# Cross attention with its reciprocal root begun inside the first query strip, delayed scores and whole sample rows; reciprocal roots by Sqrt and a reciprocal

## The chip, the cores and the metric

The kernel runs on one core of one Trainium2 chip. The engines of the core work side by side and meet only at semaphores: TensorE (PE, with its weight loads shown as PEld), VectorE (DVE), ScalarE (ACT), GpSimd (POOL) and SyncE (SP), which issues nearly all DMAs. The metric is the device time of one launch in microseconds. The kernel before took 2563.21 us, the median of three runs (2562.52 to 2563.56).

## The reference

One layer of a decoder step, on 256 prompt tokens (one sequence) and 64 sample tokens (8 sequences of 8), with d = 2048. Everything is float32.

```python
x += 0.5 * swiglu(rmsnorm(x), 5632 wide)              # ffn1
h = rmsnorm(x);  z = h @ w_in                         # 6144 columns
x += concat(hgrn2(z, 8 heads), conv_module(z)) @ w_out  # mixer; each head ends in an rmsnorm, the conv module in a layernorm
q = (rmsnorm(x) @ wq)                                 # cross attention, 4 heads of 128
s = q @ mk.T * 128**-0.5                              # 256 memory tokens
x += (softmax(s) @ mv) @ wo                           # prompt: mk, mv from mem; samples: from the caches
x += 0.5 * swiglu(rmsnorm(x), 5632 wide)              # ffn2
y = rmsnorm_final(x)
def rmsnorm(x, g): return x * rsqrt(mean(x*x) + 1e-6) * g
```

## The kernel before

Activations lie transposed: 16 tiles of 128 features by 320 tokens (256 prompt, then 64 sample). Every weight is read once. A **unit** is a 128x1024 piece of the weight stream: `load` (L134) has SP issue one 512 KB DMA into `raw` (3 buffers), then `split` (L122) makes two fp32r halves of it, `whi` by a cast on ACT (L123) and `wlo` by a subtraction on DVE (L124), 4 buffers each. `unit` fetches units until 4 are ahead of the one in use, with high priority. `mm3` (L186) then multiplies one 128x128 block: three fp32r matmuls into PSUM, L189 (whi by the high half of the activation), L190 (whi by the low half) and L191 (wlo by the high half). A **strip** (L194) is 16 such blocks, two units, 48 matmuls, into one `acc` tile (4 PSUM buffers). Small matmuls use `sm` tiles (4 more).

A scheduler sets the order of instructions on each engine, from the order of the code, priorities and its own costs. Each engine then runs its list strictly in that order: whatever stands behind an instruction that waits, waits too.

**The root.** An rmsnorm is folded in late: strips run on unnormalised x, and their result is multiplied by r = 1/sqrt(mean x² + eps). `Stat` sums squares: ACT squares each tile (L223), POOL adds it up (L225). `rstd` (L230) sums over the partitions by a matmul with ones (L232; with `tail` the last square is not added on POOL but by a second matmul, L234), and `root` (L202) makes r from it: Ln (L205), Identity for v (L206), Exp of -0.5 Ln (L207) and Square (L208) on ACT, then two DVE instructions of a Newton step (L209, L210). The same `root` is called 15 times: ffn1 (the first, called right after the head strips), the memory norm, the mixer norm, 8 heads (L720), the conv layernorm (L547), the cross attention, ffn2 and the final norm.

**Cross attention** (phase `xattn`, from L757). `qstrip(h)` runs one strip of wq; after the first it makes r, then q = acc * r (L793). The attention is fed into the strips by two queues of generators, `aq` (prompt) and `sq` (samples): `tick` counts mm3 blocks, and with `pace[0] = 2` every second block each queue advances one step (to its next `yield`). `attend(h)` is a prompt head: scores (L804), softmax (`exps`: maximum L779, Exp L782, reciprocal of the sums L785, scaling L811), transposes (L817), a copy (L821), values (L825). `attend_sample(j)` does the samples of heads 2j and 2j+1: 16 score matmuls of 32 rows (L835), in 4 steps of 4; softmax; transposes (L851); a copy (L852); 32 value matmuls (L863), in 8 steps of 4; scaling (L873) and a transpose (L876). The caches come in `kv` tiles (8 buffers): those of the second pair go into the buffers of the first as these come free, by DMAs on SP's one queue, between the loads of `raw`. After the four strips `drain` runs what is left; then the wo stage starts, 16 accumulators of 12 matmuls, each added to x by DVE (L904).

Of the kernel before, what the change touches and what calls it, by code (L numbers as in the profile page):

```python
# [13 lines left out]
AF = mybir.ActivationFunctionType  # L14
# [10 lines left out]
T = NP + NS  # L25
# [41 lines left out]
def hymba(tc, A, O):  # L67
    nc = tc.nc
# [14 lines left out]
    with (  # L83
# [11 lines left out]
        def sm():  # L95
            return tl(pp, [P, 512], F32, "sm", 4)
# [94 lines left out]
            nc.tensor.matmul(out, lo, xh, start=False, stop=last)  # L191
            tick(1)

        def strip(xg, ps):  # L194
            for half in range(2):
                w = unit()
                for kk in range(8):
                    k = half * 8 + kk
                    mm3(ps, w, kk, *xg[k], k == 0, k == KT - 1)


        def root(r, ps, n):  # L202
            v = tl(mp, [P, r.shape[-1]], F32, "sq", 2)
            a = sm()[:, : r.shape[-1]]
            nc.scalar.activation(r, ps, AF.Ln, bias=eps, scale=1.0 / n)  # L205
            nc.scalar.activation(v, ps, AF.Identity, bias=eps, scale=1.0 / n)  # L206
            nc.scalar.activation(r, r, AF.Exp, scale=-0.5)  # L207
            nc.scalar.activation(a, r, AF.Square)  # L208
            nc.vector.scalar_tensor_tensor(a, v, -0.5, a, ALU.mult, ALU.mult)  # L209
            nc.vector.scalar_tensor_tensor(r, a, 1.5, r, ALU.add, ALU.mult)  # L210
# [248 lines left out]
        with phase("mixer") as wk:  # L459
# [278 lines left out]
                pump()  # L738


            stat = Stat()
            xg = []
            for part in range(2):
                if part:
# [12 lines left out]
        with phase("xattn") as ap:  # L757
# [28 lines left out]

            def qstrip(h):
                ps = acc()
                strip(xg, ps[:, :T])
                if h == 0:  # L790
                    roots.append(stat.rstd())
                q = tl(ap, [P, T], F32, "q", XH)
                nc.vector.tensor_tensor(q, ps[:, :T], roots[0], ALU.mult)  # L793
                nc.gpsimd.tensor_copy(
                    restride(qms[h].rearrange("p a b -> p (a b)"), 0, [[128, 2], [40, 4], [1, TS]]),
                    restride(q, NP, [[32, 2], [TS, 4], [1, TS]]),
                )
                qs.append(q)
                os_.append(pair("h"))

            def attend(h):
                ps = sm()
                for j in range(2):
                    nc.tensor.matmul(  # L804
                        ps[:, j * 256 : (j + 1) * 256], qs[h][:, j * P : (j + 1) * P], kT[:, h, :], start=True, stop=True
                    )
                pr = tl(ap, [P, 2, MEM], F32, "pr", 2)
                sums = tl(ap, [P, 2], F32, "sums", 2)
                exps(ps.rearrange("p (a b) -> p a b", a=2), pr, 2, sums)
                for j in range(2):  # L810
                    nc.vector.tensor_scalar(pr[:, j, :], pr[:, j, :], sums[:, j : j + 1], None, ALU.mult)  # L811
                yield
                yield
                pt = sm()
                for mc in range(2):
                    for j in range(2):
                        nc.tensor.transpose(  # L817
                            pt[:, mc * 256 + j * P : mc * 256 + (j + 1) * P], pr[:, j, mc * P : (mc + 1) * P], ident
                        )
                pT = tl(ap, [P, 2, NP], F32, "pT", 2)  # L820
                nc.scalar.copy(pT.rearrange("p a b -> p (a b)"), pt)  # L821
                yield
                po = sm()
                for mc in range(2):
                    nc.tensor.matmul(  # L825
                        po[:, :NP], vM[:, mc, h * P : (h + 1) * P], pT[:, mc, :], start=mc == 0, stop=mc == 1
                    )
                split(os_[h][0][:, :NP], os_[h][1][:, :NP], po[:, :NP])

            def attend_sample(j):  # L830
                ps = sm()
                for i4 in range(4):
                    for c in range(4):
                        h, i = 2 * j + c // 2, (c % 2) * 4 + i4
                        nc.tensor.matmul(  # L835
                            ps[c * 32 : (c + 1) * 32, :MEM],
                            qms[h][:, i, :],
                            kv["ck", j, i // 2][:, ((i % 2) * 2 + c // 2) * MEM : ((i % 2) * 2 + c // 2 + 1) * MEM],
                            start=i4 == 0,
                            stop=i4 == 3,  # L840
                            tile_position=(0, c * 32),
                        )
                    yield
                pr = tl(ap, [P, 1, MEM], F32, "prs", 2)
                sums = tl(ap, [P, 1], F32, "sums1", 2)
                exps(ps[:, :MEM].unsqueeze(1), pr, 1, sums)
                yield
                yield
                pt = sm()
                for mc in range(2):  # L850
                    nc.tensor.transpose(pt[:, mc * P : (mc + 1) * P], pr[:, 0, mc * P : (mc + 1) * P], ident)  # L851
                nc.vector.tensor_copy(  # L852
                    restride(pm, 0, [[P, 8], [40, 4], [1, TS]]), pt[:, :256].rearrange("p (a b c) -> p a b c", a=8, b=4)
                )
                yield
                po = sm()
                for mc in range(2):
                    for i4 in range(4):
                        for c in range(4):
                            i = (c % 2) * 4 + i4  # L860
                            b = mc * 512 + c * 128 + i4 * 32
                            v0 = (i % 2) * 512 + mc * 256 + (c // 2) * P
                            nc.tensor.matmul(  # L863
                                po[c * 32 : (c + 1) * 32, :P],
                                pm[:, b : b + 32],
                                kv["cv", j, i // 2][:, v0 : v0 + P],
                                start=mc == 0 and i4 == 0,
                                stop=mc == 1 and i4 == 3,
                                tile_position=(0, c * 32),
                            )  # L870
                        yield
                on = tl(ap, [P, P], F32, "on", 1)
                nc.vector.tensor_scalar(on, po[:, :P], sums, None, ALU.mult)  # L873
                yield
                pt = sm()
                nc.tensor.transpose(pt[:, :P], on, ident)  # L876
                for c in range(2):
                    h = 2 * j + c
                    split(os_[h][0][:, NP:], os_[h][1][:, NP:], pt[:, c * 64 : (c + 1) * 64])
# [29 lines left out]
        with phase("ffn2") as fp:  # L909
            prev, stat1 = stat, Stat(True)  # L910

            def last(n):
                stat1.add(xs[n])
                nc.scalar.activation(xs[n], xs[n], AF.Copy, scale=norm("final", n))
                if n == 1:
                    warm = cp.tile([P, 1], F32, name="warm")
                    nc.scalar.activation(warm, stat1.total[:, :1], AF.Ln)

            ffn(fp, xg, prev.rstd, last)
            r = stat1.rstd()  # L920
# [151 lines left out]
```

## Time and profile before

| | |
|---|---|
| runs (three) | 2562.52, 2563.56, 2563.21 us; median 2563.21 |
| the profiled execution, its own time | 2563.12 us |
| its span, first to last instruction | 2561.3 us |
| mean granted TensorE clock | 0.996 |
| PE busy | 2530.1 us, 99% of the span, 17300 matmuls |
| DVE, ACT, POOL busy | 1458.9, 1070.1, 98.4 us |
| DMA | 393.18 MB, mean 154 GB/s |
| cross attention, strips | from 1526.1 us on |

"Busy" is the share of time in which an engine has an instruction under way. Matmuls overlap in the pipe: a row of the timeline lasts 0.31 us, but in an undisturbed stream the next one starts 0.147 us later, so the distance between starts is what to look at. In the timeline a row has its start, its duration, engine, line and tiles, and in square brackets the idle time before it with what ended it. A plain float32 matmul shows as two entries (x2). In views by stretch of time each row has, for PE, PEld, DVE, ACT and POOL, busy time and number of instructions, then the granted PE clock (1.00 is full), the DMA share and GB/s.

### The profile page before, as it was taken

What the parts mean: (1) busy time and instruction counts of PE and PEld (TensorE: products, weight loads), DVE (VectorE), ACT (ScalarE), POOL (GpSimd) and SP (SyncE); (2) the same over time, 40 slices, a digit from 0 to 9 for tenths busy, and PEclk for the clock granted to TensorE, in tenths of its full rate; (3) what the DMA queues carried; (4) which work ended last, traced back from release to release, by engine and by line L of the source; (5) the groups of instructions that cost most, each with busy time, mean ns of one, the idle gap of its engine ahead of it and who ended that gap; (6) DMA issues with size and microseconds to landing.
All of it is one profiled execution on the core that took longest, in us unless ns stands there. A gap on an engine that the chain in (4) does not pass through costs nothing.

```text
span 2561.3 us, 41649 instructions
## 1 busy us (share of the span) xinstructions
PE 2530.1 (99%) x17300; PEld 2488.9 (97%) x17300; DVE 1458.9 (57%) x2082; ACT 1070.1 (42%) x1472; POOL 98.4 (4%) x104
## 2 busy tenths in 40 slices
PE   8999999999999999999999999999999999999997
PEld 8999999999999999999999997999999999999997
DVE  7545444444444557898787675644444444444444
ACT  6433333333333355555567554533333333333334
POOL 3100000000000020000000021100000000000002
PEclk9999999999999999999999999999999999999999
DMA  6544444444444446444443554444444444444443
GB/s 217 185 148 152 151 150 148 149 150 151 151 148 149 150 154 209 153 153 149 145 151 119 164 193 146 145 152 150 149 148 150 151 152 149 149 149 152 151 149 107
DMA packets 111214, 393.18 MB, mean 154 GB/s; under 512 B 12593, under 2 KB 16817, under 8 KB 111025
## 3 DMA queue, kind: packets, MB, share of 16 engines
q1 hardware_dynamic: 110880, 390.35, 47.0%
q8 instruction: 136, 2.23, 0.3%
q14 instruction: 54, 0.43, 0.0%
q10 hardware_dynamic: 144, 0.16, 0.0%
HBM read 380.71 MB, written 9.76 MB: 152 GB/s over the span
## 4 chain that ended last, share of the span: by engine, by line
PE 95%; DVE 2%; ACT 1%; issue 1%; DMA 0%; SPq 0%; POOLq 0%; DVEq 0%; ACTq 0%
PE acc L189 30%; PE acc L190 30%; PE acc L191 30%; PE sm L612 1%; DVE xgl L243 1%; DVE wlo L124 1%; PE acc L439 1%; PE acc L441 1%; PE acc L440 1%; PE sm L671 0%; ACT whi L123 0%; DMA raw<-in_w 0%; PE sm L707 0%; ACT L207 0%; DVE x L904 0%
## 5 line engine op out<-in xcount | busy, mean ns | idle before, releaser
L123 ACT CAST whi<-raw 128x1024 fp32r<-128x1024 f32 (+1 forms) x689 | 721.7, 1048 | 1363.5 <-PE acc L190 987.5
L124 DVE TENSOR_TENSOR wlo<-raw,whi 128x1024 fp32r<-128x1024 f32 (+1 forms) x689 | 849.0, 1232 | 540.9 <-ACT whi L123 540.4
L189 PE MATMUL acc<-xgh,whi 128*128 128x320 f32 x3616 | 1130.5, 313 | 1.1 <-ACT whi L123 0.7
L191 PE MATMUL acc<-xgh,wlo 128*128 128x320 f32 x3616 | 1119.5, 310 | 1.7 <-DVE wlo L124 1.7
L190 PE MATMUL acc<-xgl,whi 128*128 128x320 f32 x3616 | 1118.8, 309 | 0.5 <-DVE xgl L243 0.4
L189 PEld LDWEIGHTS acc<-xgh,whi 128*128 128x128 f32 x3616 | 680.2, 188 | 7.3 <-issue 4.6
L191 PEld LDWEIGHTS acc<-xgh,wlo 128*128 128x128 f32 x3616 | 680.0, 188 | 2.4 <-DVE wlo L124 1.9
L190 PEld LDWEIGHTS acc<-xgl,whi 128*128 128x128 f32 x3616 | 680.3, 188 | 1.9 <-DVE xgl L243 1.0
L189 PE MATMUL acc<-hh,whi 128*128 128x320 f32 x1728 | 535.3, 310 | 2.1 <-ACT hh L123 1.3
L190 PE MATMUL acc<-hl,whi 128*128 128x320 f32 x1728 | 534.5, 309 | 2.3 <-DVE hl L124 2.3
L191 PE MATMUL acc<-hh,wlo 128*128 128x320 f32 x1728 | 534.1, 309 | 0.0
L189 PEld LDWEIGHTS acc<-hh,whi 128*128 128x128 f32 x1728 | 324.1, 188 | 5.2 <-ACT hh L123 2.8
L190 PEld LDWEIGHTS acc<-hl,whi 128*128 128x128 f32 x1728 | 324.4, 188 | 3.3 <-DVE hl L124 2.8
L191 PEld LDWEIGHTS acc<-hh,wlo 128*128 128x128 f32 x1728 | 324.3, 188 | 0.1
L288 DVE SCALAR_TENSOR_TENSOR x<-acc,x 128x320 f32<-128x320 f32 x192 | 94.1, 491 | 228.2 <-PE acc L191 228.1
L225 POOL TENSOR_TENSOR ssq<-ssq,sq 128x320 f32<-128x320 f32 x73 | 82.1, 1125 | 1867.6 <-ACT sq L223 964.6
L511 DVE SCALAR_TENSOR_TENSOR hl<-u,vec,hl 128x256 f32<-128x256 f32 x240 | 112.5, 478 | 1.8
L249 DVE TENSOR_TENSOR fa<-acc,r 128x320 f32<-128x320 f32 x87 | 42.7, 491 | 108.1 <-PE acc L191 108.0
L257 DVE TENSOR_TENSOR fb<-acc,fa 128x320 f32<-128x320 f32 x87 | 42.7, 491 | 106.9 <-PE acc L191 106.8
L251 DVE TENSOR_TENSOR fa<-fa,r 128x320 f32<-128x320 f32 x88 | 43.7, 497 | 0.1
L124 DVE TENSOR_TENSOR hl<-fb,hh 128x320 fp32r<-128x320 f32 x88 | 42.6, 484 | 0.0
L250 ACT ACTIVATE fa<-fa 128x320 f32<-128x320 f32 x88 | 40.9, 465 | 2.9 <-DVE fa L249 2.7
(208 smaller groups left out, 1055.0 us busy)
## 6 DMA issues: line engine op xcount, KB each, us to landing
raw<-in_w SPq DMA_DIRECT2D x687, 512.0 KB, 3.7
t<-in_s SPq DMA_DIRECT2D x8, 512.0 KB, 4.9
out_ss<-t SPq DMA_DIRECT2D x8, 512.0 KB, 4.1
kv<-in_ck SPq DMA_DIRECT2D x8, 512.0 KB, 5.9
kv<-in_cv SPq DMA_DIRECT2D x8, 512.0 KB, 5.9
mem<-in_mem SPq DMA_DIRECT2D x4, 512.0 KB, 7.3
x<-in_x SPq DMA_DIRECT2D x3, 640.0 KB, 8.0
out_y<-x SPq DMA_DIRECT2D x3, 640.0 KB, 3.1
```

Source lines behind the costliest of these rows:

```text
L123: nc.scalar.copy(hi, src)
L124: nc.vector.tensor_tensor(lo, src, hi.bitcast(F32), ALU.subtract)
L189: nc.tensor.matmul(out, hi, xh, start=first, stop=False)
L190: nc.tensor.matmul(out, hi, xl, start=False, stop=False)
L191: nc.tensor.matmul(out, lo, xh, start=False, stop=last)
L225: nc.gpsimd.tensor_tensor(self.total, self.total, s, ALU.add)
L249: nc.vector.tensor_tensor(t, pg[:, :T], r, ALU.mult)
L250: nc.scalar.activation(t, t, AF.Silu)
L251: nc.vector.tensor_tensor(t, t, r, ALU.mult)
L257: nc.vector.tensor_tensor(h, pu[:, :T], t, ALU.mult)
L288: nc.vector.scalar_tensor_tensor(xs[n], ps[:, :T], 0.5, xs[n], ALU.mult, ALU.add)
L511: nc.vector.scalar_tensor_tensor(dw[:, :NP], u[:, j : j + NP], cw, dw[:, :NP], ALU.mult, ALU.add)
```

## The change

`root` takes Sqrt on ACT and a reciprocal on DVE in place of Ln and Exp on ACT; the Newton step stays. In the cross attention r is made between the two halves of the first strip (with the last square added by the second matmul), the generators of the prompt heads begin 2 steps later (5 for the first), those of the samples 2 steps later, and the 16 score matmuls and 32 value matmuls of a sample pair stand in one step each. A small activation that fetches the last root's table ahead now fetches that of Sqrt.

```diff
-        def strip(xg, ps):
+        def strip(xg, ps, between=None):
             for half in range(2):
+                if half and between is not None:
+                    between()
                 w = unit()
@@ root
-            nc.scalar.activation(r, ps, AF.Ln, bias=eps, scale=1.0 / n)
+            nc.scalar.activation(r, ps, AF.Sqrt, bias=eps, scale=1.0 / n)
             nc.scalar.activation(v, ps, AF.Identity, bias=eps, scale=1.0 / n)
-            nc.scalar.activation(r, r, AF.Exp, scale=-0.5)
+            nc.vector.reciprocal(r, r)
             nc.scalar.activation(a, r, AF.Square)
             nc.vector.scalar_tensor_tensor(a, v, -0.5, a, ALU.mult, ALU.mult)
             nc.vector.scalar_tensor_tensor(r, a, 1.5, r, ALU.add, ALU.mult)
@@ statistics of the cross attention's norm
-            stat = Stat()
+            stat = Stat(True)
@@ qstrip
-                strip(xg, ps[:, :T])
-                if h == 0:
-                    roots.append(stat.rstd())
+                strip(xg, ps[:, :T], (lambda: roots.append(stat.rstd())) if h == 0 else None)
@@ attend
+                for _ in range(5 if h == 0 else 2):
+                    yield
                 ps = sm()
@@ attend_sample
+                yield
+                yield
                 ps = sm()
                 for i4 in range(4):
                     for c in range(4):
                         ...
-                    yield
@@ attend_sample, values
                 for mc in range(2):
                     for i4 in range(4):
                         ...
-                        yield
@@ last
-                    nc.scalar.activation(warm, stat1.total[:, :1], AF.Ln)
+                    nc.scalar.activation(warm, stat1.total[:, :1], AF.Sqrt)
```

The line numbers of the changed kernel are 2 higher from `root` on. The order of instructions moves at three places that the prediction speaks of.

**First root (ffn1), ACT and DVE.** `whi_513`, `wlo_514` and so on are the two halves of the next weight units, `r_482` is the root, `fa` a gate of the ffn. Before, ACT and then DVE:

```order
L205 ACT_TABLE_LOAD
L205 ACTIVATE r_482<-sm_480,eps 128x320
L206 ACTIVATE sq_483<-sm_480,eps 128x320
L207 ACT_TABLE_LOAD
L207 ACTIVATE r_482<-r_482 128x320
L208 ACTIVATE sm_484<-r_482 128x320
L123 CAST whi_513<-raw_512 128x1024
L209 SCALAR_TENSOR_TENSOR sm_484<-sq_483,sm_484 128x320
L210 SCALAR_TENSOR_TENSOR r_482<-sm_484,r_482 128x320
L249 TENSOR_TENSOR fa_491<-sm_122,r_482 128x320
L249 TENSOR_TENSOR fa_501<-acc_124,r_482 128x320
L124 TENSOR_TENSOR wlo_514<-raw_512,whi_513 128x1024
```

With the change:

```order
L207 ACT_TABLE_LOAD
L207 ACTIVATE r_482<-sm_480,eps 128x320
L208 ACTIVATE sq_483<-sm_480,eps 128x320
L123 CAST whi_513<-raw_512 128x1024
L210 ACTIVATE sm_484<-r_482 128x320
L123 CAST whi_519<-raw_518 128x1024
L209 RECIPROCAL r_482<-r_482 128x320
L124 TENSOR_TENSOR wlo_514<-raw_512,whi_513 128x1024
L211 SCALAR_TENSOR_TENSOR sm_484<-sq_483,sm_484 128x320
L124 TENSOR_TENSOR wlo_520<-raw_518,whi_519 128x1024
L212 SCALAR_TENSOR_TENSOR r_482<-sm_484,r_482 128x320
```

The cast of the next unit moved ahead of ACT's Square, and its subtraction from behind two gates to right behind the reciprocal.

**Root of the cross attention, ACT**, from the cast ahead of it to the first Exp (`pr`, `sums`). Before, and behind it the change:

```order
L123 CAST whi_15382<-raw_15381 128x1024
L205 ACT_TABLE_LOAD
L205 ACTIVATE r_15366<-sm_15364,eps 128x320
L206 ACTIVATE sq_15367<-sm_15364,eps 128x320
L207 ACT_TABLE_LOAD
L207 ACTIVATE r_15366<-r_15366 128x320
L208 ACTIVATE sm_15368<-r_15366 128x320
L123 CAST whi_15437<-raw_15436 128x1024
L782 ACTIVATE pr_15396,sums_15397<-sm_15393,mx_2274_15398 128x256 x2
```

```order
L123 CAST whi_15346<-raw_15345 128x1024
L207 ACTIVATE r_15336<-sm_15333,eps 128x320
L208 ACTIVATE sq_15337<-sm_15333,eps 128x320
L210 ACTIVATE sm_15338<-r_15336 128x320
L123 CAST whi_15382<-raw_15381 128x1024
L123 CAST whi_15412<-raw_15411 128x1024
L784 ACT_TABLE_LOAD
L784 ACTIVATE pr_15432,sums_15433<-sm_15429,mx_2277_15434 128x256
L123 CAST whi_15468<-raw_15467 128x1024
L784 ACTIVATE pr_15432,sums_15433<-sm_15429,mx_2277_15434 128x256
```

Both table loads of the root are gone here, and one for Exp has come, behind two casts and ahead of the first Exp.

**PE, the sample values.** `acc_15595` and `acc_15466` are strips. Before, a piece between two of the eight steps (each of the rows of L863 stands there twice), and then the change, where all 32 value matmuls follow one another (each of the four rows eight times):

```order
L863 MATMUL sm_15585<-kv_15283,pm 32x128
L189 MATMUL acc_15595<-xgh_14743,whi_15437 128x320
L190 MATMUL acc_15595<-xgl_14744,whi_15437 128x320
L191 MATMUL acc_15595<-xgh_14743,wlo_15438 128x320
L189 MATMUL acc_15595<-xgh_14782,whi_15437 128x320
L190 MATMUL acc_15595<-xgl_14783,whi_15437 128x320
L191 MATMUL acc_15595<-xgh_14782,wlo_15438 128x320
L863 MATMUL sm_15585<-kv_15281,pm 32x128
L863 MATMUL sm_15585<-kv_15285,pm 32x128
```

```order
L190 MATMUL acc_15466<-xgl_15212,whi_15382 128x320
L827 MATMUL sm_15568<-pT_15556,vM 128x256 x2
L866 MATMUL sm_15573<-kv_15278,pm 32x128
L866 MATMUL sm_15573<-kv_15282,pm 32x128
L866 MATMUL sm_15573<-kv_15280,pm 32x128
L866 MATMUL sm_15573<-kv_15284,pm 32x128
L191 MATMUL acc_15466<-xgh_15211,wlo_15383 128x320
```

Seven of the eight steps of the first pair, and with them seven breaks in the strip, are gone; its score matmuls (L835, now L839) went the same way, from four pieces to one. In the same list the matmuls of the root stand 24 strip matmuls earlier, with one matmul more (L236), and the first scores 9 strip matmuls later in the second strip.

## The prediction

> **What bounds the kernel now.** I read the page's first part, then PE's own waits, then the idle time of PE in stretches of 10 us over the whole span, then the timeline where a stretch had any.
>
> ```profile
> PE 2530.1 (99%) x17300; PEld 2488.9 (97%) x17300; DVE 1458.9 (57%) x2082; ACT 1070.1 (42%) x1472; POOL 98.4 (4%) x104
> PE sm L804 <- DVE q L793: 3.2, 2, 2.6
> PE acc L191 <- DVE wlo L124: 1.7, 1, 1.7
> PE acc L189 <- ACT whi L123: 0.7, 1, 0.7
> 42.80:46.50 3.70, 1.29 (x8) 1.01 (x8) 3.53 (x7) 3.67 (x5) 0.00 (x0) 1.00 0.01 2
> 46.50:49.60 3.10, 3.10 (x13) 3.10 (x13) 3.10 (x5) 1.42 (x3) 0.00 (x0) 0.50 0.84 234
> 1537.80:1540.40 2.60, 0.02 (x2) 0.02 (x1) 1.55 (x4) 1.87 (x3) 0.01 (x1) 1.00 0.19 72
> 1540.40:1545.00 4.60, 4.60 (x19) 4.50 (x20) 2.71 (x6) 1.02 (x4) 1.16 (x1) 0.63 0.33 114
> ```
>
> PE is the bound, so only time in which PE stands still or runs slowly can be won, apart from a tail after its last matmul. PE is idle for 31.2 us of 2561.3 us. Some of that is the start and the tail. Of the rest, two places hang on a root: at 42.8 us (waits of 0.7 and 1.7 us) and at 1537.8 us (2.6 us). Behind each the granted clock is low for 3 to 5 us, 0.50 and 0.63: the halt costs twice, once as a wait and once as 3.10 * 0.50 = 1.55 us and 4.60 * 0.37 = 1.70 us of lost clock.
>
> **The change, part 1: the root.** Each `root` loses an Exp, mostly its table load too, and gains a DVE reciprocal of 320 elements.
>
> ```profile
> L205 ACT ACT_TABLE_LOAD x14 | 18.0, 1283 | 0.2
> L207 ACT ACT_TABLE_LOAD x15 | 19.2, 1283 | 0.3
> L209 DVE SCALAR_TENSOR_TENSOR sm<-sq,sm 128x320 f32<-128x320 f32 x14 | 6.9, 496 | 31.0 <-ACT sm L208 30.9
> L382 DVE RECIPROCAL le<-le x1: 203/203/203, 37.5 to 37.5; 128x8 f32<-128x8 f32 x1
> L785 DVE RECIPROCAL sums<-sums x6: 163/166/167, 1543.6 to 1580.2; 128x2 f32<-128x2 f32 x4, 128x1 f32<-128x1 f32 x2
> ```
>
> The trace has reciprocals of 1, 2 and 8 elements only: 163, 166 and 203 ns. From 2 to 8 is 37 ns, 6.2 ns for each; 166 + 318 * 6.2 = 2.13 us; from 1 to 8 it is 5.7 ns, 1.99 us. I take R = 2.05 us. Bounds: 0.50 us if it runs like the other DVE work on 320 elements (496 ns), 8.1 us if all of the 203 ns grew with the size (40 * 203). The slope speaks for the middle.
>
> [...]
>
> From Sqrt to the Newton step the chain is 0.53 + R + 0.44 with two handovers, 3.1 us, against 3.23 us now (Ln at 2546.53, L209 at 2549.76 in the tail). On DVE, R falls mostly into time in which it already stood idle ahead of L209, 31.0 us over 14 roots, 2.2 us each. So roots that stand off PE's path cost nothing: the memory's, the mixer norm's, ffn2's and those of the heads. If that cover is gone, the next in line is a head's `qk` product, of which the next L612 is in want:
>
> ```profile
> 1149.09 0.48 DVE L616 TENSOR_TENSOR qk<-qk,f 128x320 f32<-128x320 f32 x1
> 1151.97 0.61 PE L612 MATMUL sm<-qk 128*128 128x128 f32 x4
> ```
>
> Here, where DVE has no gap, the product is done 2.4 us early; R pushes it to the edge, not over it. The conv norm's root has two halts behind it:
>
> ```profile
> 1397.37 0.71 PE L189 MATMUL acc<-hh,whi 128*128 128x320 f32 x3 [1.17 <-ACT hh L123]
> 1399.47 0.41 PE L190 MATMUL acc<-hl,whi 128*128 128x320 f32 x1 [1.39 <-DVE hl L124]
> ```
>
> I let it keep its time within 0.3 us: its next unit's cast and subtraction stand ahead of the Newton step now, and lose what the table load gave. I count 0, bounds -0.5 and +0.5 us.
>
> **Part 2: the first root, where the unit behind it comes earlier.**
>
> ```profile
> 39.35 0.53 ACT L205 ACTIVATE r<-sm,eps 128x320 f32<-128x320 f32 x1 [0.75 <-PE sm L232]
> 39.77 0.52 ACT L206 ACTIVATE sq<-sm,eps 128x320 f32<-128x320 f32 x1
> 42.49 1.03 ACT L123 CAST whi<-raw 128x1024 fp32r<-128x1024 f32 x1
> 42.51 0.31 PE L191 MATMUL acc<-xgh,wlo 128*128 128x320 f32 x1
> 44.52 1.22 DVE L124 TENSOR_TENSOR wlo<-raw,whi 128x1024 fp32r<-128x1024 f32 x1
> 45.79 0.41 PE L191 MATMUL acc<-xgh,wlo 128*128 128x320 f32 x1 [1.66 <-DVE wlo L124]
> ```
>
> Now the cast waits for Ln, table load, Exp and Square. With the change it follows Identity: 40.3 to 41.3. The reciprocal runs from 39.9 to 42.0, the subtraction from 42.0 to 43.2, and its first reader, due three matmul steps after 42.51 (43.0), starts at 43.25 in place of 45.79: 2.5 us won. With 0.3 us of halt left there is no slow stretch behind: another 1.5 us. **4.0 us**; bounds 0 (something else holds the unit) and 4.4 us (R = 0.5). The casts behind it are free, their units having been loaded long before (cast there without a DMA wait).
>
> **Part 3: the cross attention.**
>
> ```profile
> 1528.17 1.03 POOL L225 TENSOR_TENSOR ssq<-ssq,sq 128x320 f32<-128x320 f32 x1 [2.49 <-ACT sq L223]
> 1533.14 0.70 PE L232 MATMUL sm<-ssq,ones 128*128 128x320 f32 x2
> 1533.82 0.31 PE L190 MATMUL acc<-xgl,whi 128*128 128x320 f32 x1
> 1539.84 0.49 DVE L793 TENSOR_TENSOR q<-acc,r 128x320 f32<-128x320 f32 x1
> ```
>
> The root's matmuls move from 1533.14 to 24 steps after the strip's start, 1529.6; the last square no longer passes POOL. Sqrt 1530.8 (no table load in the list here), DVE's subtraction ahead of it until 1532.0, reciprocal until 1534.0, Square, Newton until 1535.5, the next unit's subtraction, q at 1537.3 in place of 1540.3. The scores stand 9 steps later, which with the strip before comes to 1539.5: the wait of 2.6 us ends, and the one of 0.6 us at the third head too, 9 steps more lying there as well (L804, 3.2 us in two). With them the slow stretch: 1.7 us. The new Exp table load, 1.28 us like the others, stands behind a cast at 1538 and is done before the scores' maximum (1541.4). The extra matmul of the root costs PE 0.5 us (the one now: 1533.14 to 1533.82, less a step of 0.15).
>
> The samples:
>
> ```profile
> 1550.72 0.31 PE L191 MATMUL acc<-xgh,wlo 128*128 128x320 f32 x1
> 1550.96 0.64 PE L835 MATMUL sm<-kv,qm 128*32 128x256 f32 x8
> 1551.53 0.41 PE L189 MATMUL acc<-xgh,whi 128*128 128x320 f32 x1
> 1551.78 0.30 PE L190 MATMUL acc<-xgl,whi 128*128 128x320 f32 x1
> 1576.91 1.93 PE L835 MATMUL sm<-kv,qm 128*32 128x256 f32 x32
> 1578.78 0.42 PE L189 MATMUL acc<-hh,whi 128*128 128x320 f32 x1
> 1570.81 0.43 PE L863 MATMUL sm<-kv,pm 128*32 128x128 f32 x8
> 1571.17 0.41 PE L189 MATMUL acc<-xgh,whi 128*128 128x320 f32 x1
> 1583.55 1.95 PE L863 MATMUL sm<-kv,pm 128*32 128x128 f32 x64
> 1585.43 0.41 PE L190 MATMUL acc<-hl,whi 128*128 128x320 f32 x1
> ```
>
> A piece of four scores takes 0.57 us, and the steps into and out of it 0.24 and 0.25 in place of 0.147, 0.2 us more. The second pair, which runs after the strips, already stands in one: 1.87 us for 16. Four pieces to one: 4 * 0.57 - 1.87 + 3 * 0.2 = 1.0 us. Values: 0.36 us for four, 1.88 us for 32: 8 * 0.36 - 1.88 + 7 * 0.2 = 2.4 us. Sum 3.2 + 1.7 - 0.5 + 1.0 + 2.4 = **7.8 us**. Below it lies 3 us (only the pieces, the wait replaced), above it 9 us.
>
> What is queued behind: SP now issues the four key loads and two value loads of the second pair ahead of one `raw` load, which so waits for the last of the first pair's values (some 1558 us). That load belongs to the fifth unit of the wo stage, needed after 1585; four units lie between. The wo stage paces PE by DVE (L904), and DVE starts it earlier too.
>
> **Part 4: the tail.**
>
> ```profile
> 2546.53 0.53 ACT L205 ACTIVATE r<-sm,eps 128x320 f32<-128x320 f32 x1 [0.38 <-PE sm L234]
> 2549.76 0.50 DVE L209 SCALAR_TENSOR_TENSOR sm<-sq,sm 128x320 f32<-128x320 f32 x1 [4.76 <-ACT sm L208]
> ```
>
> 3.1 us in place of 3.23: **0.1 us**; bounds by R: 1.6 us won at 0.5; lost, 0.5 at 2.67 and 6 at 8.1.
>
> **Sum.** 4.0 + 7.8 + 0.1 = 11.9 us off the profiled execution's own 2563.12 us (0.1 us below the median of the runs): 2551.2 us.
>
> **Rivals.** [...] (b) A new wait takes the place of the old one in the attention: the first Exp waits behind a cast that waits for PE's unit, and the transposes stand 27 steps into the third strip; the whole is now denser, six softmaxes without strip work to spare between. Each wait of about 1 us for four heads gives 4 us back: 2555 us. Against it: in the place now where they follow closest, the transposes did not wait for the softmax:
>
> ```profile
> 1553.15 0.66 PE L817 MATMUL sm<-ident,pr 128*128 128x128 f32 x4
> ```
> (c) The first root keeps its halt, since `raw` or the slot is not free: 2555 us. Against it: the cast ran at 42.49 without a DMA wait. (d) The other side: the reciprocal takes the heads over the edge. Slack 2.4 us with eight heads: at R = 4 us each head's PE waits 1.6 us, 13 us together, and from about there it is slower than before; at 8.1 us 2563 + 8 * 5.7 - 12 + 6 = some 2600 us. Only the bound that contradicts the slope gives that.
>
> [...]
>
> **How the numbers follow.** Forecast (2549 to 2552.5) 0.60; (a) 0.15; (b) 0.11; (c) 0.08; (d) 0.04; 0.02 for what I don't see. A change of 0.2%, 5.1 us, is about what a measurement of this kernel tells from none, so faster needs less than 2558.1 us: the forecast, (a), (c) and two thirds of (b), somewhat rounded down, 0.87; same 0.08; slower 0.05. The range reaches from R = 0.5 with both upper bounds (2547.5) to past (b) and (c) (2556.5).
>
> **What would show it.** The reciprocal's row at 2.0 to 2.1 us; no wait of L806 on q and full clock at 1540; the first root's L191 wait under 0.5 us with no stretch at 0.50; pieces of x32 and x64 for both pairs. It is wrong if the reciprocal exceeds 3 us, or PE waits for transposes or `qk`.

## The result and the profile after

The changed kernel took 2550.52 us, median of five (four lie between 2549.74 and 2552.04; the fifth took 6386.53, and without it the median would be 2550.2). The kernel before beside it: 2563.44 us. The ratio is 0.995, 95% interval 0.9938 to 0.9963: faster by 12.9 us. Forecast were 2551.2 us. The profiled execution took 2552.04 us for itself, 11.1 us less than the profiled one of before, against a sum of 11.9. That the total fits says little yet, since three of its terms turned out different. First the busy times on the page of the changed kernel:

```profile
PE 2526.3 (99%) x17302; PEld 2490.9 (98%) x17302; DVE 1485.8 (58%) x2097; ACT 1042.9 (41%) x1441; POOL 97.6 (4%) x103
```

PE's waits (total, times, longest), of which these two are the largest:

```profile
PE acc L189 <- ACT hh L123: 2.0, 1, 2.0
PE acc L190 <- DVE hl L124: 1.5, 2, 0.9
```

And the rows of the reciprocal (ns: shortest, median, longest):

```profile
L209 DVE RECIPROCAL vT<-vT x8: 2141/2147/2153, 1086.3 to 1456.4; 128x320 f32<-128x320 f32 x8
L209 DVE RECIPROCAL rmem<-rmem x1: 1753/1753/1753, 184.3 to 184.3; 128x256 f32<-128x256 f32 x1
```

The waits of L191 on `wlo` and of the scores (now L806) on `q` are gone. Those on `hh` and `hl`, most of them behind the conv norm, are left. Of 29 table loads of the root before (L205 and L207) 12 are left, and of 57 in the whole kernel 41, all of 1283 ns; the change did not add loads.

To see where the time went I timed the same strip matmuls in each trace. Of the 16128 matmuls of L189, L190 and L191, in order of start, the 120th, 300th, 8600th, 8790th, 9400th, 9900th and 16100th end the stretches. What a stretch gained or lost against the profile of before is in this table, in us; its heads give the times in the profile of before, and the sum is the difference of the spans.

| profile | start, to 26.5 | first root, to 59.3 | to 1388.0 | conv norm, to 1428.3 | to 1524.8 | attention and wo, to 1630.5 | ffn2, to 2540.1 | tail | sum |
|---|---|---|---|---|---|---|---|---|---|
| predicted | 0 | -4.0 | 0 | 0 | 0 | -7.8 | 0 | -0.1 | -11.9 |
| the change | +1.2 | -4.2 | -0.7 | +2.6 | 0.0 | -9.9 | 0.0 | 0.0 | -11.0 |
| again | +0.8 | -4.2 | -0.7 | +1.0 | 0.0 | -9.9 | 0.0 | 0.0 | -12.9 |
| root_only | +1.0 | -4.1 | -0.7 | +1.4 | 0.0 | -6.5 | 0.0 | 0.0 | -8.9 |
| xattn_only | +0.6 | -0.1 | 0.0 | 0.0 | 0.0 | -10.0 | 0.0 | +0.1 | -9.5 |
| pieces | +1.0 | -4.2 | -0.7 | 0.0 | 0.0 | -3.6 | 0.0 | 0.0 | -7.6 |
| late_r | +0.4 | -4.2 | -0.7 | +2.7 | 0.0 | -10.4 | 0.0 | 0.0 | -12.3 |
| no_delay | +0.1 | -4.2 | -0.7 | +2.3 | 0.0 | -8.9 | 0.0 | 0.0 | -11.4 |
| conv_ln | +1.4 | -4.1 | -0.7 | +1.6 | 0.0 | -9.9 | 0.0 | 0.0 | -11.8 |
| conv_warm | +0.3 | -4.1 | -0.7 | -0.7 | 0.0 | -9.9 | 0.0 | 0.0 | -15.1 |
| root_rows | +0.9 | -4.2 | -0.7 | 0.0 | 0.0 | -10.4 | 0.0 | 0.0 | -14.4 |
| recip2_heads | +0.3 | -4.1 | +0.2 | -0.7 | +0.9 | -9.9 | 0.0 | 0.0 | -13.4 |
| conv_warm2 | +0.9 | -4.2 | -0.6 | -1.1 | 0.0 | -9.8 | 0.0 | 0.0 | -14.9 |
| rows_warm | +0.1 | -4.1 | -0.7 | -0.7 | 0.0 | -10.4 | 0.0 | +0.1 | -15.8 |

In the start every kernel runs the same instructions in the same order, so its 0.1 to 1.4 us belong to the execution and not to an edit.

The first root went as predicted. In the timeline of the changed kernel (start, duration, instruction) the reciprocal, the subtraction and its first reader follow one another:

```profile
41.01 2.15 DVE L209 RECIPROCAL r<-r 128x320 f32<-128x320 f32 x1 [1.69 <-ACT r L207]
43.08 1.16 DVE L124 TENSOR_TENSOR wlo<-raw,whi 128x1024 fp32r<-128x1024 f32 x1
43.91 0.31 PE L190 MATMUL acc<-xgl,whi 128*128 128x320 f32 x1
44.30 0.41 PE L191 MATMUL acc<-xgh,wlo 128*128 128x320 f32 x1
```

PE stands 0.24 us (44.30 less 43.91 less the step of 0.15) where it stood 2.4 us, and no slow stretch follows (granted clock 1.00 from 39.0 to 49.6 us). What nobody forecast is the stretch behind the conv norm. By stretches of time (PE, PEld, DVE, ACT and POOL busy, then the granted clock), the changed kernel and then its second run:

```profile
1392.20:1394.30 2.10, 0.05 (x5) 0.01 (x1) 1.86 (x5) 2.09 (x5) 0.00 (x0) 1.00 0.01 2
1394.80:1401.60 6.80, 6.22 (x24) 6.01 (x23) 3.42 (x8) 6.78 (x17) 0.00 (x0) 0.50 0.22 77
```

```profile
1391.90:1394.00 2.10, 0.06 (x4) 0.00 (x0) 1.85 (x5) 2.09 (x5) 0.00 (x0) 1.00 0.02 6
1394.40:1397.70 3.30, 2.83 (x12) 2.45 (x11) 2.20 (x6) 3.30 (x9) 0.00 (x0) 0.51 0.43 139
```

The same halt of 2.1 us is followed by half clock for 6.8 us in the one execution and for 3.4 us in the other (6.83 and 3.41 us in the clock records of the traces). Before, the halts of 1.2 and 1.4 us had none behind them (clock 1.00 up to 1406 us).

### The profile page after: what moved, and what is told of

It is laid out like the page before. It is cut to its first block, busy times and chain, and to the rows that moved or that the text cites. A ratio compares the mean times of both kernels' runs of the same rounds, so it can differ in the third digit from the quotient of the medians.

```text
span 2550.2 us, 41620 instructions
## 1 busy us (share of the span) xinstructions
PE 2526.3 (99%) x17302; PEld 2490.9 (98%) x17302; DVE 1485.8 (58%) x2097; ACT 1042.9 (41%) x1441; POOL 97.6 (4%) x103
## 4 chain that ended last, share of the span: by engine, by line
PE 96%; DVE 2%; ACT 1%; issue 1%; DMA 0%; SPq 0%; POOLq 0%; DVEq 0%; ACTq 0%
PE acc L189 30%; PE acc L190 30%; PE acc L191 30%; PE sm L614 1%; DVE xgl L245 1%; DVE wlo L124 1%; PE acc L441 1%; PE acc L443 1%; PE acc L442 1%; PE sm L673 0%; DMA raw<-in_w 0%; ACT whi L123 0%; PE sm L709 0%; PE sm L721 0%; DVE x L906 0%
## 5 line engine op out<-in xcount | busy, mean ns | idle before, releaser
L189 PE MATMUL acc<-xgh,whi 128*128 128x320 f32 x3616 | 1128.6, 312 | 0.4 <-DVE x L906 0.4
L191 PE MATMUL acc<-xgh,wlo 128*128 128x320 f32 x3616 | 1118.5, 309 | 0.1
L190 PE MATMUL acc<-xgl,whi 128*128 128x320 f32 x3616 | 1118.0, 309 | 0.5 <-DVE xgl L245 0.4
L189 PEld LDWEIGHTS acc<-xgh,whi 128*128 128x128 f32 x3616 | 679.5, 188 | 3.9 <-issue 2.2
L190 PEld LDWEIGHTS acc<-xgl,whi 128*128 128x128 f32 x3616 | 679.4, 188 | 1.9 <-DVE xgl L245 1.0
L191 PEld LDWEIGHTS acc<-xgh,wlo 128*128 128x128 f32 x3616 | 679.0, 188 | 0.6 <-DVE wlo L124 0.3
L189 PE MATMUL acc<-hh,whi 128*128 128x320 f32 x1728 | 536.2, 311 | 2.1 <-ACT hh L123 2.0
L190 PE MATMUL acc<-hl,whi 128*128 128x320 f32 x1728 | 536.1, 310 | 1.5 <-DVE hl L124 1.5
L191 PE MATMUL acc<-hh,wlo 128*128 128x320 f32 x1728 | 535.2, 310 | 0.0
L189 PEld LDWEIGHTS acc<-hh,whi 128*128 128x128 f32 x1728 | 325.2, 188 | 4.2 <-ACT hh L123 2.8
L190 PEld LDWEIGHTS acc<-hl,whi 128*128 128x128 f32 x1728 | 325.5, 188 | 2.7 <-DVE hl L124 2.0
L191 PEld LDWEIGHTS acc<-hh,wlo 128*128 128x128 f32 x1728 | 325.5, 188 | 0.3 <-issue 0.2
```

What stands on the lines that cost most here:

```text
L189: nc.tensor.matmul(out, hi, xh, start=first, stop=False)
L190: nc.tensor.matmul(out, hi, xl, start=False, stop=False)
```

## The experiments

Each kernel was timed five times (pieces seven) beside the kernel before, whose medians there lay between 2562.53 and 2563.09 us. The names are those of the table.

### The change once more

No edit.

> The changed kernel once more, as the partner of the others. Theory: about 2550.5 us; its first profile had 1.2 us of lost clock in the head strips (before 25 us), which the kernel before did not have there, and 2.8 us more than the kernel before around the conv norm (clock 0.50 behind one wait of 2.05 us). If the first is chance and the second belongs to the change, this profile has the second and perhaps not the first; if both are chance, neither, and the time is nearer 2548 us.

Measured: 2549.92 us (2548.51 to 2550.22), ratio 0.9949 (0.9936 to 0.9961). The halt at the conv norm was the same and its slow stretch half as long, as shown above: +1.0 in place of +2.6 us. So the halt belongs to the change, and the length of the slow stretch to the execution.

### The root alone

```diff
 (the kernel before)
-            nc.scalar.activation(r, ps, AF.Ln, bias=eps, scale=1.0 / n)
+            nc.scalar.activation(r, ps, AF.Sqrt, bias=eps, scale=1.0 / n)
...
-            nc.scalar.activation(r, r, AF.Exp, scale=-0.5)
+            nc.vector.reciprocal(r, r)
...
-                    nc.scalar.activation(warm, stat1.total[:, :1], AF.Ln)
+                    nc.scalar.activation(warm, stat1.total[:, :1], AF.Sqrt)
```

> The kernel before with only the new root (Sqrt and reciprocal, and the table fetched ahead for the tail). Theory of separate terms: first root -4.1 us, heads -0.7, conv norm +2.8 (its two halts become one, and the clock falls behind it), cross attention -0.6 (no table loads, but a reciprocal), tail -0.1: 2563.3 - 2.7 = 2560.6 us. Rival: the conv norm's loss in the first profile belongs to the other edits or to chance, then 2557.9 us.

Measured: 2553.53 us (2553.19 to 2554.14), ratio 0.9964 (0.9952 to 0.9977): 9.0 us won, against 2.7 expected. Both theories were wrong, and at the same place: the attention won 6.5 us. The timeline of this kernel, r and the first scores:

```profile
1530.67 0.70 PE L232 MATMUL sm<-ssq,ones 128*128 128x320 f32 x2
1532.95 2.15 DVE L207 RECIPROCAL r<-r 128x320 f32<-128x320 f32 x1
1537.53 0.49 DVE L210 SCALAR_TENSOR_TENSOR r<-sm,r 128x320 f32<-128x320 f32 x1
1538.05 0.89 DVE L793 TENSOR_TENSOR q<-acc,r 128x320 f32<-128x320 f32 x2
1538.69 1.04 PE L804 MATMUL sm<-kT,q 128*128 128x256 f32 x4
```

Here r is made where it always was, behind the first strip, and it is 7.4 us from L232 to the product of q (L793), against 6.7 before (1533.14 to 1539.84). So q does not come earlier, it comes later. But PE waits for nothing: the scheduler has put the first scores 8.0 us behind L232 in PE's list, with some 50 strip matmuls between, where before they were due 4.7 us behind it (1537.80). The only wait of the scores on q that is left is that of the third head, 0.6 us. With the halt its slow stretch went too (clock 1.00 from 1524 to 1590 us), and the list also has the first pair's 16 score matmuls in one row of 1.93 us. The two table loads that the old root needs take 2 * 1.283 = 2.57 us, and the old halt was 2.58 us. That the scheduler's costs leave the loads out would explain it; it was argued from these two numbers, not tested.

### The cross attention alone

```diff
 (the changed kernel)
-            nc.scalar.activation(r, ps, AF.Sqrt, bias=eps, scale=1.0 / n)
+            nc.scalar.activation(r, ps, AF.Ln, bias=eps, scale=1.0 / n)
...
-            nc.vector.reciprocal(r, r)
+            nc.scalar.activation(r, r, AF.Exp, scale=-0.5)
 (and Ln in the small activation near the end)
```

> The changed kernel with Ln and Exp again in every root: only the edits in the cross attention are left. Theory of separate terms: q comes about 1 us later than with the new root but is due 2.4 us after it was ready, so the whole 9.4 us stays: 2553.9 us, with the halt at 43 us back and two short halts at the conv norm without a slow stretch. Rival: early r needs the new root to be in time, the scores wait again about 1 us or more: 2556 us.

Measured: 2553.55 us (2551.34 to 2553.95), ratio 0.9961 (0.9947 to 0.9974). As the theory said. The attention and wo win all of their 10.0 us, with q (L793 at 1536.85) in time for its scores, and the halts elsewhere are those of before. So the root alone is worth 9.0 us and the attention alone 9.0, but both together 12.6: some 5.4 us are counted twice. Both end the same halt ahead of the first scores with the slow stretch behind it (2.6 + 1.7 us), and both bring the first pair's scores into one row (1.0 us).

### Sample rows in pieces again

```diff
 (the changed kernel)
                             tile_position=(0, c * 32),
                         )
+                    yield
                 pr = tl(ap, [P, 1, MEM], F32, "prs", 2)
...
                                 tile_position=(0, c * 32),
                             )
+                        yield
                 on = tl(ap, [P, P], F32, "on", 1)
```

> The changed kernel with the samples' score and value matmuls in four and eight steps again. Theory: the breaks in the stream cost what the first pair showed before, 1.0 + 2.4 us: 2553.9 us; it may be up to 1 us more, since the transposes of a prompt head then break the stream apart from the samples. Rival: the gain of the cross attention came from the ended waits and the clock alone, and the breaks cost nothing on the way to the end: 2550.5 us.

Measured: 2555.84 us (2555.23 to 2556.46), ratio 0.9973 (0.9962 to 0.9984). The pieces cost 5.9 us, where 3.4 had been worked out. They don't only break the stream. The second pair also ends in waits of its own, as PE's waits of this kernel show:

```profile
PE sm L867 <- DVE pm L856: 0.5, 1, 0.5
PE sm L880 <- DVE on L877: 0.5, 1, 0.5
```

PE idles 1.3 us of 1570 to 1580 here, and nowhere in the attention of the changed kernel.

### r behind the strip, and no delays

```diff
 (late_r: the changed kernel with)
-            stat = Stat(True)
+            stat = Stat()
...
-                strip(xg, ps[:, :T], (lambda: roots.append(stat.rstd())) if h == 0 else None)
+                strip(xg, ps[:, :T])
+                if h == 0:
+                    roots.append(stat.rstd())
 (no_delay: the changed kernel with)
-                for _ in range(5 if h == 0 else 2):
-                    yield
...
-                yield
-                yield
                 ps = sm()
                 for i4 in range(4):
```

> The changed kernel with r of the cross attention made after the first strip again, the last square added on POOL. Theory: the root begins 24 matmul steps (3.5 us) later and passes POOL; q, ready at 1536.05 in the changed kernel, comes at 1539.6 or later, and the scores, which stood at 1538.42, wait 1.2 to 1.5 us; one matmul less gives 0.5 us back, no slow stretch behind a halt this short: 2551.4 us. Rival: the delayed scores alone cover it: 2550.0 us. Other rival: POOL and a cast ahead push q by 2 us more, halt over 2.5 us with a slow stretch: 2555 us.

> The changed kernel without the delayed first steps of the prompt and sample generators. Theory: for the first head the early r alone is enough (q ready at 1536.05, scores then due at 1537.1), the later heads wait about 0.6 us for q where one waited so before, and the transposes may stand before their softmax: +1 to +2 us, 2552 us. Rival: the delay does nothing: 2550.5 us. Other rival: the first scores wait again for over 2 us, with the clock behind it: 2554 us or more.

Measured: late_r 2549.79 us (2548.13 to 2550.86), ratio 0.9945 (0.9933 to 0.9958); no_delay 2551.38 us (2550.81 to 2551.76), ratio 0.9953 (0.9939 to 0.9966). The early r is worth nothing here: late_r is as fast as the change, its attention 0.5 us shorter, without a wait on q. From its timeline, q and the first scores:

```profile
1533.55 2.14 DVE L209 RECIPROCAL r<-r 128x320 f32<-128x320 f32 x1
1538.66 0.89 DVE L795 TENSOR_TENSOR q<-acc,r 128x320 f32<-128x320 f32 x2
1539.30 1.04 PE L808 MATMUL sm<-kT,q 128*128 128x256 f32 x4
```

Without the delays the attention is 1.0 us longer than in the change (8.9 us won in place of 9.9). The rest of the 1.5 us is not told apart from the conv norm's slow stretch, which made that stretch 2.3 us longer in this profile.

### The root and the rows, nothing else

```diff
 (the kernel before, with the three lines of root_only and)
                             tile_position=(0, c * 32),
                         )
-                    yield
                 pr = tl(ap, [P, 1, MEM], F32, "prs", 2)
...
                                 tile_position=(0, c * 32),
                             )
-                        yield
                 on = tl(ap, [P, P], F32, "on", 1)
```

> The kernel before with the new root and the sample rows in one step each, but without the early r and without the delays. Theory after the first runs: the new root by itself ended the halt ahead of the first scores, and early r and delays are a second remedy for the same halt; then this is within 1.5 us of the changed kernel, 2550 to 2551.5 us, with a cross attention 8.5 to 9.5 us shorter than before. Rival: each edit has a share of its own, and the shares of r and delays (2 to 3 us) are missing: 2552.5 us or more.

Measured: 2549.32 us (2548.73 to 2550.16), ratio 0.9948 (0.9935 to 0.996). It has neither the early r nor the delays, and is as fast as the whole change; its attention is as short as that of late_r (-10.4). Against root_only the rows won 4.0 us in the attention and 4.2 us in the time.

### A head's reciprocal done twice

```diff
 (the changed kernel; root is called with twice=True from the eight heads)
+            if twice:
+                nc.vector.reciprocal(a, r)
             nc.vector.reciprocal(r, r)
```

> The changed kernel with the reciprocal of the eight heads' roots done twice (a first one whose result is overwritten), so that a head's root costs DVE 4.3 us in place of 2.15. Theory of the prediction (the slower side): slack of a head's qk product 2.4 us, so PE waits 1.6 to 1.9 us in each head: 2550 + 13 to 15 = 2563 to 2565 us. Rival: the order is made anew with the longer root in view, the qk product is put ahead of the Newton steps, and DVE has idle time enough: 2550 to 2552 us.

Measured: 2551.63 us (2549.78 to 2552.18), ratio 0.9956 (0.9943 to 0.9968). Eight more reciprocals of 2.15 us, 17 us of DVE, cost 1.7 us, and PE waits 0.6 us on `qk` in two heads, not in eight. The added reciprocal and these waits:

```profile
L210 DVE RECIPROCAL sm<-vT x8: 2152/2155/2161, 1085.4 to 1454.1; 128x320 f32<-128x320 f32 x8
```

```profile
PE sm L616 <- DVE qk L620: 0.6, 2, 0.3
```

The `qk` product (L620) stands ahead of the second Newton step (L214) in this list. A slack read from the old order is not the slack of a new one.

### The conv norm: Ln again, or Silu's table fetched early

```diff
 (conv_ln: the changed kernel; root is called with ln=True from the conv norm)
-            nc.scalar.activation(r, ps, AF.Sqrt, bias=eps, scale=1.0 / n)
+            nc.scalar.activation(r, ps, AF.Ln if ln else AF.Sqrt, bias=eps, scale=1.0 / n)
...
-            nc.vector.reciprocal(r, r)
+            if ln:
+                nc.scalar.activation(r, r, AF.Exp, scale=-0.5)
+            else:
+                nc.vector.reciprocal(r, r)
 (conv_warm: the changed kernel; root is called with silu=True from the conv norm)
             nc.vector.reciprocal(r, r)
+            if silu:
+                nc.scalar.activation(a[:, :1], v[:, :1], AF.Silu)
 (conv_warm2: conv_warm, and in the loop over the squares of the conv norm)
                         nc.vector.tensor_tensor(vs, vs, s, ALU.add)
+                        if c == NC - 1:
+                            nc.scalar.activation(prev[:, :1], prev[:, :1], AF.Sqrt)
+                        prev = s
```

The small activations write a column that is overwritten or not read again.

> The changed kernel with Ln and Exp in the conv norm's root alone. Theory: its two halts of 1.2 and 1.4 us come back in place of one of 2.05 us and a short one, the clock stays full, and the 2.8 us are won: 2547.7 us. Rival: the slow stretch does not hang on the length of a single halt but on the new order around it or on chance: 2550.5 us.

> The changed kernel with a one-column Silu on ACT right behind the Identity of the conv norm's root, so that Silu's table is loaded while ACT waits for the reciprocal. Theory: the load of 1.28 us leaves the chain from the root to the first Silu, and the next unit's cast too; the halt of 2.05 us falls to 0.8 us or less, the clock stays full: 2546.5 us. Rival: the low half of the split becomes the wait, because DVE has all eight products ahead of it: 2549.5 us with a halt of 1 to 2 us on the low half.

> The changed kernel with the early Silu table load of the conv norm (the run conv_warm) and a one-column Sqrt ahead of the matmul of the conv norm's root, so that Sqrt's table is loaded while ACT is idle for 2.1 us. Theory: the chain begins 1.1 us earlier, the halt of 1.5 us falls to about 0.4, and no halt is left that could cost a window of slow clock there: 2547 us, and less spread than conv_warm (2547.9 to 2550.0). Rival: DVE, with its eight products and the low halves, sets the start, the halt stays over 1 us: 2548 us.

Measured: conv_ln 2550.14 us (2548.61 to 2551.37), ratio 0.9947 (0.9935 to 0.996); conv_warm 2548.03 us (2547.85 to 2550.04), ratio 0.9942 (0.993 to 0.9955); conv_warm2 2548.47 us (2547.89 to 2549.78), ratio 0.9946 (0.9932 to 0.996).

conv_ln won nothing. Its two halts are those of the kernel before, to 0.01 us, and yet a slow stretch stands behind them:

```profile
1393.96 0.70 PE L189 MATMUL acc<-hh,whi 128*128 128x320 f32 x3 [1.18 <-ACT hh L123]
1396.07 0.41 PE L190 MATMUL acc<-hl,whi 128*128 128x320 f32 x1 [1.40 <-DVE hl L124]
```

```profile
1396.60:1400.00 3.40, 3.40 (x15) 3.40 (x14) 2.00 (x5) 3.40 (x9) 0.00 (x0) 0.50 0.47 153
```

So the theory that one long halt slows the clock and two short ones don't has fallen. In the profile of pieces the reverse is seen: the halts of the changed kernel, and full clock behind them.

```profile
1392.00:1394.00 2.00, 0.02 (x3) 0.00 (x0) 1.75 (x5) 1.99 (x5) 0.00 (x0) 1.00 0.01 2
1395.20:1401.00 5.80, 5.63 (x40) 5.63 (x41) 2.79 (x7) 5.78 (x14) 0.00 (x0) 1.00 0.28 90
```

Like halts had 0, 3.4 or 6.8 us of half clock behind them: whole multiples of 3.41 us. The clock records of the traces show where these begin. Every stretch of full or half clock that a trace holds begins on one grid of 3.413 us steps; in the change half clock begins at 12.46 and at 1394.86 us, 405 such steps apart, and in the kernel before at 46.51 and 1541.55 us, 438 apart. Where the grid lies differs from one execution to the next: a step begins at 1394.86 us in the change and at 1396.61 us in conv_ln, half a step later. Cut along the grid of its own trace, the stretch or the two that hold the halts look like this in the change, conv_ln, pieces (two) and the kernel before (two):

```profile
1391.45:1394.86 3.41, 1.36 (x21) 0.82 (x19) 3.17 (x7) 3.40 (x6) 0.00 (x0) 1.00 0.14 52
1393.19:1396.61 3.42, 1.24 (x6) 0.99 (x7) 3.42 (x8) 3.42 (x8) 0.00 (x0) 1.00 0.24 78
1389.69:1393.11 3.42, 2.33 (x29) 1.88 (x28) 3.42 (x10) 2.81 (x4) 0.00 (x0) 1.00 0.46 153
1393.11:1396.52 3.41, 1.86 (x11) 1.60 (x12) 2.85 (x5) 3.41 (x8) 0.00 (x0) 1.00 0.10 36
1394.77:1398.18 3.41, 2.14 (x26) 1.43 (x24) 3.41 (x10) 3.40 (x6) 0.00 (x0) 1.00 0.48 154
1398.18:1401.59 3.41, 2.12 (x14) 2.12 (x15) 2.93 (x6) 3.41 (x9) 0.00 (x0) 1.00 0.36 118
```

The next step ran at half clock behind the first two, in which PE was busy for 1.36 and 1.24 of 3.41 us, and at full clock behind the others, busy for 1.86 to 2.33 us, in which the grid had split the halt. All 14 traces agree between the first matmuls and the tail: behind a full-clock step with 1.8 us or more of idle PE came half clock, behind one with 1.56 us or less full clock, and in between it went either way (1.67 us in root_only, slow; 1.69 us in root_rows, full). So in these traces the cost of like halts hung on where the grid happened to lie: 2.05 us inside one step had 6.8 us of half clock behind it (the change), the same 2.05 us split over two steps none (pieces), and the full clock behind the halts of before was luck too. Why a second slow step follows in some traces (the change, late_r, no_delay) and not in others stays open. No single long wait was needed: half clock came behind 2.05 us in one piece (the change), and also behind 1.18 and 1.40 us in two (conv_ln).

conv_warm makes the halt itself shorter. ACT of the changed kernel, and then of conv_warm:

```profile
1387.77 0.43 ACT L210 ACTIVATE sm<-mu 128x320 f32<-128x320 f32 x1
1390.49 0.48 ACT L599 COPY ket<-sm 128x384 f32<-128x384 f32 x1 [2.29 <-PE sm L597]
1390.99 1.28 ACT L553 ACT_TABLE_LOAD   x1
1392.29 0.65 ACT L553 ACTIVATE hl<-hl,vec 128x320 f32<-128x320 f32 x1
```

```profile
1385.49 1.28 ACT L211 ACT_TABLE_LOAD   x1
1386.78 0.17 ACT L211 ACTIVATE sm<-sq 128x1 f32<-128x1 f32 x1
...
1392.89 0.70 PE L189 MATMUL acc<-hh,whi 128*128 128x320 f32 x3 [1.54 <-ACT hh L123]
```

The load now runs while DVE has the reciprocal (in conv_warm2 the load starts at 1384.69 us, and the reciprocal runs from 1384.68 for 2.15 us). PE waits 1.54 us, then for nothing up to 1402 us, and the stretch is 3.3 us shorter than in the first profile of the change (-0.7 for +2.6). Part of that is the clock's luck: against the second run of the change the stretch is 1.7 us shorter and the median time 1.9 us. conv_warm2 cut the halt to 0.95 us, but 0.86 us of wait on the low half came back behind it, much as its rival had it, and the time is the same.

### What pays, put together

```diff
 (root_rows, with the Silu line of conv_warm in root, for the conv norm)
```

> The kernel before with only what the runs showed to pay: the new root, the sample rows in one step each, and the one-column Silu that loads the conv norm's next table early; no early r, no delays. Theory: the run root_rows less what conv_warm won on the changed kernel (2.0 us): 2547.3 us, its profile with a halt of about 1.5 us at the conv norm and without a slow stretch there. Rival: that gain was the luck of the slow windows in those executions: 2549.3 us.

Measured: 2547.63 us (2547.22 to 2547.68), ratio 0.994 (0.9926 to 0.9953), the fastest of all: 2.9 us under the changed kernel's first median and 15.5 us under the kernel before. All five runs lie within 0.5 us, the two sets of the change within 1.7 and 2.3 us, and against root_rows the line with Silu is worth 1.7 us without an overlap of the runs. At the conv norm the clock is full:

```profile
1390.00:1392.00 2.00, 1.05 (x21) 0.61 (x18) 2.00 (x4) 1.96 (x3) 0.00 (x0) 1.00 0.78 244
1392.00:1394.00 2.00, 1.41 (x8) 1.24 (x9) 2.00 (x6) 2.00 (x6) 0.00 (x0) 1.00 0.25 68
```

## Why the prediction was right, and where it was not

**The reciprocal's price.** R was taken as 2.05 us from three short rows and is 2.147; from 256 to 320 elements it grows by (2147 - 1753) / 64 = 6.2 ns for each, the very slope of the short rows. No run shows the 2.67 us in the tail's bounds, nor a slower reciprocal, to which the chances give 0.15 as (a): the rows of 320 elements took 2.141 to 2.153 us.

**First root.** 4.0 us predicted, 4.2 measured, by the mechanism named: 0.24 us of halt left (0.25 predicted), no slow stretch. xattn_only, where only the root is missing, has the old time back to 0.1 us.

**Heads.** The step by which R "pushes it to the edge, not over it" (the `qk` product) missed the sign. The slack of 2.4 us was read at one head, while another already waited on that product before:

```profile
1098.23 0.68 PE L612 MATMUL sm<-qk 128*128 128x128 f32 x4 [0.49 <-DVE qk L616]
```

With the change this wait went, and the stretch to 1388.0 is 0.7 us shorter, all of it around that wait. Even a doubled reciprocal does not do what rival (d) says: its 13 us were 1.7.

**Conv norm.** This step failed: 0 us with bounds of 0.5. The halts together stayed as they were (1.17 + 1.39 before, 2.05 + 0.58 after), so the waits were costed rightly. What was left out is that halts of this size cost clock in some executions: the stretch came out 0 to 2.7 us longer in the profiles with like halts. The first part of the prediction had charged 1.6 and 1.7 us of lost clock to the two other halts, and took it for certain there and for nothing here.

**Cross attention.** 7.8 us predicted, 9.9 measured. From the two traces, 4.0 us of the 9.9 are idle time of PE (4.85 us before, 0.87 after), 1.7 us are the slow clock that is gone (0.63 granted from 1540.4 to 1545.0 us before, 1.00 from 1541.0 to 1545.6 after), and the other 4.2 us are breaks in the stream, less the extra matmul; predicted were 3.2, 1.7 and 2.9. The causes were wrong in part. The 3.2 us of waits with 1.7 us of clock were put down to the early r and the delays. The step that failed is "The scores stand 9 steps later, which with the strip before comes to 1539.5: the wait of 2.6 us ends". The place came out (1538.42 us in the changed kernel, which runs 1.1 us ahead of before at that point), and xattn_only shows that these edits do end the wait. But they are not needed: root_rows, without either, wins as much as the change, since the new root makes the scheduler put the scores later by itself. The rows were put at 1.0 + 2.4 = 3.4 us and are worth 4.0 us (root_rows against root_only) to 5.9 us (the change against pieces). Only the breaks of the first pair were counted, not the waits that the pieces leave behind. Once the new root is in, the early r costs its matmul and wins nothing. Rival (b) did not happen; PE has no wait in the attention.

**The new Exp load** was to be over ahead of the scores' maximum. It is not:

```profile
1539.48 0.69 DVE L781 TENSOR_REDUCE mx<-sm 128x2 f32<-128x512 f32 x1 [0.46 <-PE sm L806]
1540.45 1.28 ACT L784 ACT_TABLE_LOAD   x1 [2.70 <-DVE mx L782]
1541.75 0.47 ACT L784 ACTIVATE pr<-sm,mx 128x256 f32<-128x256 f32 x1
```

The load waits for what its activation waits for, though ACT had been idle for 2.7 us. It cost PE nothing here: the transposes follow at 1545.12 us, and PE has no wait for the softmax.

**Tail.** 0.1 us predicted; from Sqrt to the first product with r it is 4.28 us (2535.48 to 2539.76), and before, from Ln, 4.29 (2546.53 to 2550.82): nothing.

So the total came out near the forecast partly by luck: the attention won 2.1 us more than its term and the heads 0.7, while the conv norm and the start lost 3.8 us in that one execution.

## What to carry to other kernels

Where a scheduler sets the order, an edit's effect is not its local saving: two remedies for one halt don't add up, and a change of one instruction's engine can move the reader as well. Try each edit alone, and keep only what pays; here two of the edits could be left out, and one line on a table load was worth some 2 us. A halt of PE had a second price here, in clock, which varied between executions of one kernel (6.8 and 3.4 us at half clock behind the same 2.05 us). Such a halt is best ended, or cut as in rows_warm (1.54 us, full clock), and a single profile is a poor judge of it.

## What was not expected of the hardware

Between the first matmuls and the tail, the half clock of these 14 traces came in stretches of 3.41 us or twice that, on a grid that lay anew in each execution: behind every full-clock step with 1.8 us or more of idle PE, and behind none with 1.56 us or less. So whether it came behind a halt of 2 to 2.6 us differed between executions of like code (none in pieces and root_rows, 3.4 us in the second run of the change, 6.8 us in the first). An idle ACT did not fetch the next activation table by itself: at the first Exp of the attention the load waited 2.7 us for what the Exp waits for, and at the conv norm it stood behind a copy that had waited 2.29 us. And the two table loads of a root were 2.57 us (1.283 us each) against a halt of 2.58 us that followed it; whether the scheduler leaves them out of its costs stays open.
